# fp32 products in the long convolutions of a two-block network, low parts of keys copied by ScalarE, and another hand-out of the filter's tap tiles

## The chip, the cores and the metric

One core of a Trainium2 chip runs the whole program. The metric is device time in microseconds of one execution. TensorE (PE) multiplies, VectorE (DVE) and ScalarE (ACT) do elementwise work, GpSimd (POOL) does a few additions, and all loads and stores are issued by the queue of SyncE (SP). A run with the profiler gives a trace with one record per instruction.

## The reference

Two blocks of two layers each, in fp32, for 512 tokens and 256 context tokens of width 1024. What bears on the change is in the first block's layer 0: beside attention, half of the width goes through a "Hyena" operator, a gated long convolution of order 2:

```python
z = u[0]                                    # 512 channels
for o in range(HYENA_ORDER):                # 2 orders
    k = filters[o] / norm                   # taps in both directions, from a small MLP
    z = gate[o] * (fft_conv(z, k[o]) + skip[o] * z)
```

The kernel makes the convolution with products with cosine and sine matrices, for the 512 tokens and again for the 256 context tokens. The keys of all attentions (also in the second block) are rotated, normalised and multiplied with queries in the usual way.

## The kernel before, in words

An fp32 number is held as two `float32r` tiles: `h`, a rounded copy that ACT makes (`split`, L54), and `lo`, the rest that DVE makes (L55). One fp32-like product is then three matmuls (`mm3`, L81 to L83: high by high, high by low, low by high). A few products are single matmuls on plain fp32 tiles: `ada` (L161), `hy_mlp` (L466), the column sums in `hy_taps` (L556), `neigh` (L1027), and the transposes (L87).

Tiles come from rings by tag: `a` has 24 buffers, `oa` 6, `u` 4 (each holds two 1024-column halves), `st` 4 (landing place of weights that are then split), `e` 6, `va` 4. A new tile waits until a buffer of its ring is released. The tile framework orders the instructions of each engine, and each engine then runs its own in that order; all DMAs stand in one queue, that of SP. `merge` interleaves two generators in proportion to the costs that they yield, so the order of the program is set by these written-out costs.

Layer 0 (`layer0`, L826) has these stages around the change:

- Filters, 0 to 260 us: `hy_mlp`, `hy_kernels(1)` (context) and `hy_kernels(0)`, interleaved with `inputs` (norms, transposes, and `hy_in`, 12 weight units that go through the `u` ring). `hy_kernels` calls `hy_taps` for (o, hf) = (0,0), (0,1), (1,0), (1,1), and after each but the first the `hy_spec` of the one before it. `hy_taps` makes the tap tiles `E`: for the 512-token filter and hf 0 (of both orders) four tiles from `oa`, else two from `u`. `hy_spec` reads them, and they are released after it. `oa` also gives `new_y`: two tiles `yx` and one `yc`, written at L647 from `hy_in` unit 8 on.
- Projections and attention, 260 to 480 us. `k_pair` (L103) turns a pair of key heads in PSUM into `h` and `l` tiles with each head's rows in both halves of the partitions. For each head: two copies on ACT (L106, L107) and two subtractions on DVE (L108, L109). It is called 26 times in the whole kernel, to 2520 us.
- `hyena(1, ...)` (context) interleaved with the last gates, then `hyena(0, ...)` interleaved with `ctx_out` (the context's output projection, its norm and transposes, and two chunks of `ada`), 480 to 650 us. `hyena` (L663) loads z into `st` and splits it (L674), loads the DFT matrices into `st` and splits them (`dft`, L504; into `a` for the forward ones and one `u` each for the two inverse ones), and then for each order and each frequency block: forward products into PSUM tag `S` (L689, L691), sums and differences (L692, L693), the product with the filter's spectrum (L697 to L701), sum and difference of the two halves (L707) and the split of each (L708). Then the inverse products: order 0 at L724 with the matrix as stationary operand, times the gate (L726) and split into the next z (L727); order 1 at L740, with z-blocks as stationary operand.
- `out_proj` of the 512 tokens, from 645 us on, then layer 1 and the second block.

Of the kernel before, what the change touches and what calls it, by code (L numbers as in the profile page):

```python
# [9 lines left out]
F = mybir.dt.float32  # L10
R = mybir.dt.float32r
I32 = mybir.dt.int32
OP = mybir.AluOpType
AF = mybir.ActivationFunctionType
AX = mybir.AxisListType
P = 128
# [11 lines left out]
class Net:  # L28
# [74 lines left out]
    def k_pair(self, ps, Ah, Al, Bh, Bl):  # L103
        a, v = self.nc.scalar, self.nc.vector
        for s, h, l in ((slice(0, 64), Ah, Al), (slice(64, 128), Bh, Bl)):
            a.activation(h[0:64], ps[s], AF.Copy)  # L106
            a.activation(h[64:128], ps[s], AF.Copy)  # L107
            v.tensor_tensor(l[0:64], ps[s], h[s].bitcast(F), op=OP.subtract)  # L108
            v.tensor_tensor(l[64:128], ps[s], h[s].bitcast(F), op=OP.subtract)  # L109

    def av4(self, o, blocks, first, last):

# [403 lines left out]
    def hy_taps(self, o, hf, ni, w3, C):  # L516

        nc, I = self.nc, self.I
        b0, nb = ((0, 4), (4, 2))[ni]
        n = nb * P  # L520
        hs = self.hst
        wh, wl = w3
        ch = slice(hf * 256, (hf + 1) * 256)
        if ni == 0 and hf == 0:
            E = [self.t('oa', [P, 2, 2, 256], R) for _ in range(nb)]
        else:
            ts = [self.t('u', [P, 2, 2, 2, 256], R) for _ in range(nb // 2)]
            E = [ts[b // 2][:, b % 2] for b in range(nb)]
        acc = self.t('ec', [P, 2, 256])
        for b in range(nb):  # L530
            d = C['dec'][b // 2][:, b % 2, ch]
            ps = self.ps('S')
            for j in range(2):
                c = slice((b0 + b) * P, (b0 + b + 1) * P)
                p = ps[:, j * 256:(j + 1) * 256]
                nc.tensor.matmul(p, hs[:, c], wh[:, j, ch], start=True, stop=False)
                nc.tensor.matmul(p, hs[:, c], wl[:, j, ch], start=False, stop=b > 0)
                if b == 0:

# [24 lines left out]
        nc.scalar.activation(y, y, AF.Copy, scale=-0.5 / n)  # L564
        C[o, hf, ni] = E, y
        yield 1.5
# [67 lines left out]
    def hy_in(self, w, i0, streams):  # L634
# [3 lines left out]
        for m in range(12):  # L638
            u = self.wu(w, i0 + m)
            for h, nt, ctx, y in streams:  # L640
# [19 lines left out]
                    nc.sync.dma_start(self.zscr[ctx][m // 4][:, :, cs], v.rearrange("p (b c) -> p b c", c=P))  # L660
                yield 5.6 * nt / 4

    def hyena(self, ctx, y):  # L663

        nc = self.nc
        n = 256 if ctx else 512
        nh = n // 256
        nb = 2 * nh
        zs_ = []
        for b2 in range(nh):  # L670
            st = self.t('st', [P, 2, 512])
            hi, lo = self.t('a', [P, 2, 512], R), self.t('a', [P, 2, 512], R)
            nc.sync.dma_start(st, self.zscr[ctx][0][:, 2 * b2:2 * b2 + 2])
            self.split(hi, lo, st)  # L674
            zs_.append((hi, lo))
        for o in range(2):
            F4 = [self.dft(j) for j in range(2)] if n == 512 else [self.dft(4)]
            UV = []
            inv = [self.dft(2 + j, 'u') for j in range(2)] if n == 512 else F4 * 2
            for fb in range(nh):  # L680
                K, K1 = self.t('a', [P, 2, 512]), self.t('a', [P, 2, 512])
                for j, k in enumerate((K, K1)):
                    nc.sync.dma_start(k, self.kscr[2 if ctx else fb, o, j])

                def z(b):
                    return zs_[b // 2][0][:, b % 2], zs_[b // 2][1][:, b % 2]
                Z, Z1 = self.t('a', [P, 2, 512]), self.t('a', [P, 2, 512])
                for j in range(2):
                    B = self.dft_fwd(n, 2 * j + 1, fb, z, F4)  # L689
                    nc.scalar.activation(Z1[:, j], B, AF.Copy)  # L690
                    A = self.dft_fwd(n, 2 * j, fb, z, F4)  # L691
                    nc.vector.tensor_tensor(Z[:, j], A, Z1[:, j], op=OP.add)  # L692
                    nc.vector.tensor_tensor(Z1[:, j], A, Z1[:, j], op=OP.subtract)  # L693
                yield 5.1 * nh / 2
                for z_, k in ((Z1, K1), (Z, K)):
                    t1, t2 = self.t('e', [P, 512]), self.t('e', [P, 512])
                    nc.vector.tensor_tensor(t1, z_[:, 0], k[:, 1], op=OP.mult)  # L697
                    nc.vector.tensor_tensor(t2, z_[:, 1], k[:, 0], op=OP.mult)
                    nc.vector.tensor_tensor(z_, z_, k, op=OP.mult)
                    nc.vector.tensor_tensor(z_[:, 0], z_[:, 0], z_[:, 1], op=OP.subtract)  # L700
                    nc.vector.tensor_tensor(z_[:, 1], t1, t2, op=OP.add)  # L701
                uv = []
                for cs in range(2):
                    h, lo = self.t('a', [P, 2, 512], R), self.t('a', [P, 2, 512], R)
                    for j, op in enumerate((OP.add, OP.subtract)):
                        v = self.t('e', [P, 512])
                        nc.vector.tensor_tensor(v, Z[:, cs], Z1[:, cs], op=op)  # L707
                        self.split(h[:, j], lo[:, j], v)  # L708
                    uv.append((h, lo))
                UV.append(uv)  # L710

            if o == 0:
                zn = [(self.t('a', [P, 2, 512], R), self.t('a', [P, 2, 512], R)) for _ in range(nh)]
                for b in range(nb):
                    par, hf = b // nh, b % nh
                    p1 = self.t('va', [P, 512])
                    nc.sync.dma_start(p1, self.zscr[ctx][1][:, b])
                    ps = self.ps('S')
                    for fb in range(nh):
                        for cs in range(2):  # L720
                            u = inv[cs]
                            c = (fb * 2 + par) * 256 + hf * P if n == 512 else 512 + cs * 256 + par * P
                            h, lo = UV[fb][cs]
                            self.mm3(ps, u[0][:, c:c + P], u[1][:, c:c + P], h[:, par], lo[:, par],  # L724
                                     cs == 0 and fb == 0, cs == 1 and fb == nh - 1)
                    nc.vector.tensor_tensor(p1, ps, p1, op=OP.mult)  # L726
                    self.split(zn[b // 2][0][:, b % 2], zn[b // 2][1][:, b % 2], p1)  # L727
                    yield 2.6 * nh / 2
                zs_ = zn
            else:  # L730
                w2 = n // 2
                for cb in range(4):
                    ps = self.ps('pt')
                    ch = slice(cb * P, (cb + 1) * P)
                    for fb in range(nh):
                        for cs, par in ((0, 0), (0, 1), (1, 0), (1, 1)):
                            u = inv[cs]
                            c = (fb * 2 + par) * 256 if n == 512 else 512 + cs * 256 + par * P
                            h, lo = UV[fb][cs]
                            self.mm3(ps[:, par * w2:(par + 1) * w2], h[:, par, ch], lo[:, par, ch],  # L740
                                     u[0][:, c:c + w2], u[1][:, c:c + w2], fb + cs + par == 0, fb == nh - 1 and cs + par == 2)
                    yt = y[cb // 2][:, cb % 2].rearrange("p (t two) -> p two t", two=2)
                    nc.vector.tensor_tensor(yt, ps[:, :n].rearrange("p (two t) -> p two t", two=2), yt, op=OP.mult)
                    yield 2.6 * nh / 2
# [1472 lines left out]
```

## Time and profile before

| | us |
|---|---|
| median of 3 runs | 2936.05 (2933.27 to 2937.53) |
| the profiled execution | 2934.61 |
| its span, first to last instruction | 2932.8 |
| TensorE busy | 2795.8 (95%), 14904 matmuls |
| VectorE busy | 1974.4 (67%) |
| ScalarE busy | 1383.5 (47%) |
| mean granted clock of TensorE | 0.986 |

A matmul's record lasts longer than it holds the array, since its way through the array overlaps the next one's; the distance from start to start in a dense row of like matmuls is what one costs. An fp32 matmul on plain tiles stands in the trace as two records. In the tables of the profile "idle before" is the time that an engine sat idle ahead of such instructions, and behind the arrow stands what ended it.

### The profile page before, as it was taken

Reading aid. Unit: us, or ns where it says so; the run is one execution under the profiler, and the core shown is the slowest. Engines: PE = TensorE matmul, PEld = TensorE weight load, DVE = VectorE, ACT = ScalarE, POOL = GpSimd, SP = SyncE. Lnnn points to the kernel's source line nnn. Section 1 sums busy time; section 2 is a strip of 40 time slices with the busy share of each in tenths; the row PEclk is TensorE's granted clock in tenths of the full one; section 3 lists DMA queues with packets and bytes.
Section 4 is the critical chain, followed back from the end, with each engine's and each line's share of the span. In section 5 each row is a group of like instructions: output and inputs, shape, how many; then the busy total and the mean of one; then the engine's idle time right before and its main releaser. Section 6 shows DMA issues by size and latency. Waiting matters only on the chain.

```text
span 2932.8 us, 40392 instructions
## 1 busy us (share of the span) xinstructions
PE 2795.8 (95%) x14904; PEld 2278.0 (78%) x14904; DVE 1974.4 (67%) x4467; ACT 1383.5 (47%) x2843; POOL 124.6 (4%) x182
## 2 busy tenths in 40 slices
PE   7999999889999899999999899999999999899998
PEld 3888847558898687877788788888787778788886
DVE  5768868986978747876847734346877764954445
ACT  5544565334466625655635422234566543632322
POOL 0000000111001120100000000000100000000000
PEclk8999999999999999999999999999999999999999
DMA  6443142653214232222143222223221124233321
GB/s 230 137 127 96 39 130 94 207 187 114 75 62 138 78 129 79 87 73 65 58 152 101 80 101 94 86 101 122 68 94 58 58 79 144 87 95 107 101 94 65
DMA packets 117645, 299.77 MB, mean 102 GB/s; under 512 B 21471, under 2 KB 48031, under 8 KB 117448
## 3 DMA queue, kind: packets, MB, share of 16 engines
q1 hardware_dynamic: 117448, 297.19, 31.3%
q8 instruction: 118, 1.93, 0.3%
q14 instruction: 79, 0.65, 0.1%
HBM read 273.54 MB, written 27.54 MB: 103 GB/s over the span
## 4 chain that ended last, share of the span: by engine, by line
PE 75%; DVE 15%; ACT 5%; issue 2%; DMA 2%; SPq 0%; POOL 0%; ACTq 0%; DVEq 0%
PE mm L82 17%; PE mm L81 17%; PE mm L83 17%; PE pt L87 6%; DVE u L55 2%; PE o L121 2%; PE o L122 2%; PE o L161 1%; PE S L83 1%; PE S L81 1%; PE S L82 1%; PE mm L161 1%; PE o L1027 1%; DVE a L55 1%; PE S L1633 1%
## 5 line engine op out<-in xcount | busy, mean ns | idle before, releaser
L81 PE MATMUL mm<-a,u 128*128 128x512 f32 (+1 forms) x1596 | 592.6, 372 | 3.1 <-ACT a L54 1.4
L82 PE MATMUL mm<-a,u 128*128 128x512 f32 (+1 forms) x1596 | 591.3, 371 | 0.7 <-DVE a L55 0.7
L83 PE MATMUL mm<-a,u 128*128 128x512 f32 (+1 forms) x1596 | 588.8, 369 | 1.0 <-DVE u L55 1.0
L54 ACT ACTIVATE u<-st 128x1024 fp32r<-128x1024 f32 x352 | 369.0, 1051 | 383.3 <-PE mm L83 333.1
L55 DVE TENSOR_TENSOR u<-st,u 128x1024 fp32r<-128x1024 f32 x352 | 432.0, 1229 | 141.7 <-ACT u L54 135.9
L81 PE MATMUL mm<-u,a 128*128 128x512 f32 (+1 forms) x1280 | 458.9, 359 | 7.7 <-DVE v L778 3.2
L82 PE MATMUL mm<-u,a 128*128 128x512 f32 (+1 forms) x1280 | 458.7, 358 | 4.1 <-DVE u L55 4.0
L83 PE MATMUL mm<-u,a 128*128 128x512 f32 (+1 forms) x1280 | 457.2, 357 | 0.2 <-DVE a L58 0.2
L81 PEld LDWEIGHTS mm<-a,u 128*128 128x128 f32 x1596 | 301.5, 189 | 52.5 <-ACT a L54 2.4
L83 PEld LDWEIGHTS mm<-a,u 128*128 128x128 f32 x1596 | 301.4, 189 | 49.1 <-DVE u L55 1.8
L82 PEld LDWEIGHTS mm<-a,u 128*128 128x128 f32 x1596 | 301.7, 189 | 47.8 <-issue 2.1
L81 PEld LDWEIGHTS mm<-u,a 128*128 128x128 f32 x1280 | 242.6, 190 | 44.3 <-DVE v L778 3.5
L82 PEld LDWEIGHTS mm<-u,a 128*128 128x128 f32 x1280 | 242.8, 190 | 39.8 <-DVE u L55 6.4
L83 PEld LDWEIGHTS mm<-u,a 128*128 128x128 f32 x1280 | 242.7, 190 | 34.5 <-DVE a L58 1.0
L55 DVE TENSOR_TENSOR va<-pt,va 128x512 fp32r<-128x512 f32 (+2 forms) x252 | 165.3, 670 | 67.2 <-ACT va L54 55.1
L1207 DVE SCALAR_TENSOR_TENSOR a<-a,mm 128x512 f32<-128x512 f32 x96 | 65.7, 685 | 210.3 <-PE mm L83 210.2
L87 PE MATMUL pt<-c_ident,e 128*128 128x128 f32 x1132 | 188.4, 278 | 18.7 <-DVE e L274 3.7
L54 ACT ACTIVATE va<-pt 128x512 fp32r<-128x512 f32 (+2 forms) x252 | 143.2, 583 | 122.7 <-PE pt L87 113.0
L87 PEld LDWEIGHTS pt<-c_ident,e 128*128 128x128 f32 x1132 | 133.7, 141 | 65.3 <-issue 20.4
L1892 DVE TENSOR_TENSOR v<-v 128x512 f32<-128x512 f32 x64 | 44.3, 693 | 160.4 <-ACT v L1891 159.9
L1891 ACT ACTIVATE v<-mm 128x512 f32<-128x512 f32 x60 | 36.0, 600 | 203.0 <-PE mm L83 203.0
L82 PE MATMUL S<-u,a 128*128 128x256 f32 x312 | 91.0, 292 | 1.5 <-DVE u L55 1.5
(424 smaller groups left out, 4827.7 us busy)
## 6 DMA issues: line engine op xcount, KB each, us to landing
st<-in_up SPq DMA_DIRECT2D x64, 512.0 KB
st<-in_dn SPq DMA_DIRECT2D x64, 512.0 KB
st<-in_w SPq DMA_DIRECT2D x52, 512.0 KB
st<-in_ada SPq DMA_DIRECT2D x48, 512.0 KB
st<-in_gate SPq DMA_DIRECT2D x48, 512.0 KB
st<-in_win SPq DMA_DIRECT2D x42, 512.0 KB
st<-in_wout SPq DMA_DIRECT2D x24, 512.0 KB
st<-in_br SPq DMA_DIRECT2D x16, 512.0 KB
```

The lines of the kernel that those rows point to most:

```text
L54: nc.scalar.activation(hi, src, AF.Copy)
L55: (eng or nc.vector).tensor_tensor(lo, src, hi.bitcast(F), op=OP.subtract)
L81: mm(ps, ah, bh, start=first, stop=False)
L82: mm(ps, ah, bl, start=False, stop=False)
L83: mm(ps, al, bh, start=False, stop=last)
L87: self.nc.tensor.transpose(dst, src, self.ident[:n, :n])
L121: nc.tensor.matmul(o, v, ph[:nk], start=first and bi == 0, stop=False)
L122: nc.tensor.matmul(o, v, pl[:nk], start=False, stop=last and bi == len(blocks) - 1)
L161: nc.tensor.matmul(ps[:nr], cc[:, 2 * kk + j], v[:, j * 512:(j + 1) * 512], start=kk + j + x == 0, stop=2 * kk + j == 7 and x == len(w) - 1)
L1207: self.nc.vector.scalar_tensor_tensor(xx, xx, alpha, ps, op0=OP.mult, op1=OP.add, **kw)
L1891: nc.scalar.activation(r, ps, AF.Relu)
L1892: nc.vector.tensor_tensor(sq, r, r, op=OP.mult)
```

## The change

Three edits. In `hyena`, z, the DFT matrices, the two halves of the spectrum product and the next z are kept as plain fp32 tiles without a split, and each `mm3` there becomes one matmul on fp32 tiles (`dft_fwd32` for the forward one). The loads go straight into the tiles that the matmuls read; both inverse matrices share one `u` tile. `hy_spec` keeps `dft`, `dft_fwd` and `mm3`. In `k_pair`, the second subtraction of each head becomes an ACT copy of the first one's result into the other half of the partitions. In `hy_taps`, of the 512-token filter only (0,1) takes its tap tiles from `oa`; (0,0) and (1,0), which did before, take two `u` tiles each, and (0,1), which took `u`, no longer does.

```diff
@@ k_pair
-            v.tensor_tensor(l[0:64], ps[s], h[s].bitcast(F), op=OP.subtract)
-            v.tensor_tensor(l[64:128], ps[s], h[s].bitcast(F), op=OP.subtract)
+            v.tensor_tensor(l[s], ps[s], h[s].bitcast(F), op=OP.subtract)
+            a.activation(l[64 - s.start:128 - s.start], l[s].bitcast(F), AF.Copy)
@@ hy_taps
-        if ni == 0 and hf == 0:
+        if ni == 0 and (o, hf) == (0, 1):
             E = [self.t('oa', [P, 2, 2, 256], R) for _ in range(nb)]
@@ new
+    def dft_raw(self, j):
+        t_ = self.t('a', [P, 1024])
+        self.nc.sync.dma_start(t_, self.I['dft'][j])
+        return t_
+    def dft_pair(self):
+        u = self.t('u', [P, 2, 1024])
+        for j in range(2):
+            self.nc.sync.dma_start(u[:, j], self.I['dft'][2 + j])
+        return [u[:, 0], u[:, 1]]
+    def dft_fwd32(self, n, m, fb, z, F4, ps=None):
...
+        for hf in range(nh):
...
+            self.nc.tensor.matmul(ps, u[:, c:c + P], z(par * nh + hf), start=hf == 0, stop=hf == nh - 1)
+        return ps
@@ hyena
-            st = self.t('st', [P, 2, 512])
-            hi, lo = self.t('a', [P, 2, 512], R), self.t('a', [P, 2, 512], R)
-            nc.sync.dma_start(st, self.zscr[ctx][0][:, 2 * b2:2 * b2 + 2])
-            self.split(hi, lo, st)
-            zs_.append((hi, lo))
+            z_ = self.t('a', [P, 2, 512])
+            nc.sync.dma_start(z_, self.zscr[ctx][0][:, 2 * b2:2 * b2 + 2])
+            zs_.append(z_)
...
-            F4 = [self.dft(j) for j in range(2)] if n == 512 else [self.dft(4)]
+            F4 = [self.dft_raw(j) for j in ((0, 1) if n == 512 else (4,))]
-            inv = [self.dft(2 + j, 'u') for j in range(2)] if n == 512 else F4 * 2
+            inv = self.dft_pair() if n == 512 else F4 * 2
...
-                    B = self.dft_fwd(n, 2 * j + 1, fb, z, F4)
+                    B = self.dft_fwd32(n, 2 * j + 1, fb, z, F4)
...
-                    h, lo = self.t('a', [P, 2, 512], R), self.t('a', [P, 2, 512], R)
+                    v = self.t('a', [P, 2, 512])
                     for j, op in enumerate((OP.add, OP.subtract)):
-                        v = self.t('e', [P, 512])
-                        nc.vector.tensor_tensor(v, Z[:, cs], Z1[:, cs], op=op)
-                        self.split(h[:, j], lo[:, j], v)
+                        nc.vector.tensor_tensor(v[:, j], Z[:, cs], Z1[:, cs], op=op)
...
-                            self.mm3(ps, u[0][:, c:c + P], u[1][:, c:c + P], h[:, par], lo[:, par],
-                                     cs == 0 and fb == 0, cs == 1 and fb == nh - 1)
-                    nc.vector.tensor_tensor(p1, ps, p1, op=OP.mult)
-                    self.split(zn[b // 2][0][:, b % 2], zn[b // 2][1][:, b % 2], p1)
+                            nc.tensor.matmul(ps, u[:, c:c + P], UV[fb][cs][:, par],
+                                             start=cs == 0 and fb == 0, stop=cs == 1 and fb == nh - 1)
+                    nc.vector.tensor_tensor(zn[b // 2][:, b % 2], ps, p1, op=OP.mult)
...
-                            self.mm3(ps[:, par * w2:(par + 1) * w2], h[:, par, ch], lo[:, par, ch],
-                                     u[0][:, c:c + w2], u[1][:, c:c + w2], fb + cs + par == 0, fb == nh - 1 and cs + par == 2)
+                            nc.tensor.matmul(ps[:, par * w2:(par + 1) * w2], UV[fb][cs][:, par, ch], u[:, c:c + w2],
+                                             start=fb + cs + par == 0, stop=fb == nh - 1 and cs + par == 2)
```

## Rows read from the trace of the kernel before

**Rows 1.** The page: busy time of each engine, share of the span, instructions

```profile
...
PE 2795.8 (95%) x14904; PEld 2278.0 (78%) x14904; DVE 1974.4 (67%) x4467; ACT 1383.5 (47%) x2843; POOL 124.6 (4%) x182
...
```

**Rows 2.** Busy time by engine (x instructions), PEclk, DMA share, GB/s; the hyena stretch

```profile
...
500.00:650.00 150.00, 127.08 (x532) 83.22 (x530) 138.81 (x198) 63.14 (x95) 17.44 (x8) 0.94 0.58 199
...
```

**Rows 3.** The chain of waits of 500 to 660 us, shares by line

```profile
...
by line: DVE a L55 7.4%; DVE u L55 7.3%; issue 7.0%; DMA st<-in_wout 6.8%; PE o L161 6.3%; DVE a L699 5.0%; DVE e L707 4.7%; DVE a L700 3.8%; DMA a<-kscr 3.7%; DVE e L698 3.2%; DVE e L697 3.1%; DVE a L58 2.9%; PE S L83 2.8%; PE mm L82 2.6%;
...
```

**Rows 4.** Groups by line and form, 480 to 650 us: splits

```profile
...
L55 DVE TENSOR_TENSOR u<-st,u 128x1024 fp32r<-128x1024 f32 x15 | 19.3, 1293 | 3.6 <-ACT u L54 3.5
...
L55 DVE TENSOR_TENSOR a<-e,a 128x512 fp32r<-128x512 f32 x24 | 17.7, 777 | 1.4 <-ACT a L54 1.4
...
L54 ACT ACTIVATE a<-e 128x512 fp32r<-128x512 f32 x24 | 14.8, 629 | 34.2 <-DVE e L707 34.2
...
L55 DVE TENSOR_TENSOR a<-st,a 128x1024 fp32r<-128x1024 f32 x7 | 8.4, 1216 | 0.0
...
L55 DVE TENSOR_TENSOR a<-va,a 128x512 fp32r<-128x512 f32 x6 | 6.2, 1044 | 0.0
...
```

**Rows 5.** The same view: first matmul of each three-part product in hyena

```profile
...
L81 PE MATMUL S<-a,a 128*128 128x512 f32 x44 | 19.3, 442 | 2.5 <-ACT a L54 2.4
...
L81 PE MATMUL pt<-u,a 128*128 128x256 f32 x32 | 10.0, 315 | 8.9 <-ACT a L54 8.3 <-DVE oa L743 0.7
...
L81 PE MATMUL S<-a,u 128*128 128x512 f32 x16 | 6.1, 404 | 0.0
...
L81 PE MATMUL pt<-a,a 128*128 128x128 f32 x16 | 4.4, 283 | 0.9 <-ACT a L54 0.9
...
```

**Rows 6.** Timeline of TensorE: start, length, line, tiles, form; dense rows of like matmuls

```profile
...
103.97 1.02 PE L556 MATMUL o<-ec,ones 128*128 128x256 f32 x4
...
110.32 0.28 PE L82 MATMUL mm<-a,u 128*128 128x256 f32 x1
110.44 0.28 PE L83 MATMUL mm<-a,u 128*128 128x256 f32 x1
...
515.76 7.03 PE L161 MATMUL o<-st,c 128*2 128x512 f32 x16 [0.68 <-ACT v L165]
...
527.34 0.28 PE L82 MATMUL pt<-a,a 128*128 128x128 f32 x1
527.45 0.28 PE L81 MATMUL pt<-a,a 128*128 128x128 f32 x1
...
556.16 0.39 PE L82 MATMUL mm<-u,a 128*128 128x512 f32 x1
556.39 0.39 PE L83 MATMUL mm<-u,a 128*128 128x512 f32 x1
...
949.87 1.09 PE L1027 MATMUL o<-va,a 128*64 128x128 f32 x8
...
```

**Rows 7.** Waits, 600 to 650 us: who, for whom, total us, times, longest

```profile
...
PE pt L81 <- ACT a L54: 8.3, 1, 8.3
...
```

**Rows 8.** Timeline of VectorE at the last split in hyena

```profile
...
637.84 0.69 DVE L55 TENSOR_TENSOR a<-e,a 128x512 fp32r<-128x512 f32 x1 [0.70 <-ACT a L54]
...
```

**Rows 9.** DMA queue: start, time in the queue; four DFT loads of order 1

```profile
...
565.30 17.56 SPq L507 DMA_DIRECT2D st<-in_dft  x4
...
```

**Rows 10.** Waits, 570 to 600 us, columns as in Rows 7

```profile
...
ACT u L54 <- PE mm L83: 11.1, 2, 10.6
...
```

**Rows 11.** Line L109 of k_pair: durations in ns min/median/max; who waited for it

```profile
...
L109 DVE TENSOR_TENSOR a<-pt,a x28: 417/428/695, 269.6 to 1007.4; 64x256 fp32r<-64x256 f32 x20, 64x512 fp32r<-64x512 f32 x8
...
  PEld mm L81: 3.4, 4
...
```

**Rows 12.** Line L107, the second copy of k_pair on ScalarE

```profile
...
L107 ACT ACTIVATE a<-pt x28: 375/378/593, 268.3 to 1006.6; 64x256 fp32r<-64x256 f32 x20, 64x512 fp32r<-64x512 f32 x8
...
```

**Rows 13.** End of the filters, columns as in Rows 2

```profile
...
220.00:230.00 10.00, 7.16 (x41) 6.60 (x41) 8.01 (x13) 6.02 (x11) 0.00 (x0) 0.73 0.28 68
...
```

**Rows 14.** Timeline of ScalarE: the gate unit that waits for its oa tile

```profile
...
232.80 0.78 ACT L647 ACTIVATE oa<-mm,c_hyc 128x512 f32<-128x512 f32 x1 [1.98 <-PE S L83]
```

More of the change, by code (lines that the diff above doesn't have):

```diff
@@ L661, in hy_in @@
                 yield 5.6 * nt / 4
+    def dft_raw(self, j):
[8 more added lines that the diff above has]
+    def dft_fwd32(self, n, m, fb, z, F4, ps=None):
+        par, sin = m % 2, m // 2
+        if ps is None:
+            ps = self.ps('S')
+        nh = n // 256
+        for hf in range(nh):
+            if n == 512:
+                u, c = F4[sin], (par * 2 + hf) * 256 + fb * P
+            else:
+                u, c = F4[0], sin * 256 + par * P
+            self.nc.tensor.matmul(ps, u[:, c:c + P], z(par * nh + hf), start=hf == 0, stop=hf == nh - 1)
+        return ps
     def hyena(self, ctx, y):
@@ L685, in z @@
                 def z(b):
-                    return zs_[b // 2][0][:, b % 2], zs_[b // 2][1][:, b % 2]
+                    return zs_[b // 2][:, b % 2]
                 Z, Z1 = self.t('a', [P, 2, 512]), self.t('a', [P, 2, 512])
                 for j in range(2):
-                    B = self.dft_fwd(n, 2 * j + 1, fb, z, F4)
+                    B = self.dft_fwd32(n, 2 * j + 1, fb, z, F4)
                     nc.scalar.activation(Z1[:, j], B, AF.Copy)
-                    A = self.dft_fwd(n, 2 * j, fb, z, F4)
+                    A = self.dft_fwd32(n, 2 * j, fb, z, F4)
                     nc.vector.tensor_tensor(Z[:, j], A, Z1[:, j], op=OP.add)
@@ L703, in hyena @@
                 for cs in range(2):
-                    h, lo = self.t('a', [P, 2, 512], R), self.t('a', [P, 2, 512], R)
+                    v = self.t('a', [P, 2, 512])
                     for j, op in enumerate((OP.add, OP.subtract)):
-                        v = self.t('e', [P, 512])
-                        nc.vector.tensor_tensor(v, Z[:, cs], Z1[:, cs], op=op)
-                        self.split(h[:, j], lo[:, j], v)
-                    uv.append((h, lo))
+                        nc.vector.tensor_tensor(v[:, j], Z[:, cs], Z1[:, cs], op=op)
+                    uv.append(v)
                 UV.append(uv)
             if o == 0:
-                zn = [(self.t('a', [P, 2, 512], R), self.t('a', [P, 2, 512], R)) for _ in range(nh)]
+                zn = [self.t('a', [P, 2, 512]) for _ in range(nh)]
                 for b in range(nb):
@@ L722, in hyena @@
                             c = (fb * 2 + par) * 256 + hf * P if n == 512 else 512 + cs * 256 + par * P
-                            h, lo = UV[fb][cs]
-                            self.mm3(ps, u[0][:, c:c + P], u[1][:, c:c + P], h[:, par], lo[:, par],
-                                     cs == 0 and fb == 0, cs == 1 and fb == nh - 1)
-                    nc.vector.tensor_tensor(p1, ps, p1, op=OP.mult)
-                    self.split(zn[b // 2][0][:, b % 2], zn[b // 2][1][:, b % 2], p1)
+                            nc.tensor.matmul(ps, u[:, c:c + P], UV[fb][cs][:, par],
+                                             start=cs == 0 and fb == 0, stop=cs == 1 and fb == nh - 1)
+                    nc.vector.tensor_tensor(zn[b // 2][:, b % 2], ps, p1, op=OP.mult)
                     yield 2.6 * nh / 2
@@ L738, in hyena @@
                             c = (fb * 2 + par) * 256 if n == 512 else 512 + cs * 256 + par * P
-                            h, lo = UV[fb][cs]
-                            self.mm3(ps[:, par * w2:(par + 1) * w2], h[:, par, ch], lo[:, par, ch],
-                                     u[0][:, c:c + w2], u[1][:, c:c + w2], fb + cs + par == 0, fb == nh - 1 and cs + par == 2)
+                            nc.tensor.matmul(ps[:, par * w2:(par + 1) * w2], UV[fb][cs][:, par, ch], u[:, c:c + w2],
+                                             start=fb + cs + par == 0, stop=fb == nh - 1 and cs + par == 2)
                     yt = y[cb // 2][:, cb % 2].rearrange("p (t two) -> p two t", two=2)
```

## The prediction, made before the changed kernel was seen

> **What bounds the kernel now.** I read the page first: over the whole span TensorE is busy 95%, VectorE 67%, ScalarE 47% [rows 1]. By that alone, work added to TensorE would be added to the end. But the kernel has stages with different limits, so I next read busy time by stretches. In the 150 us that hold most of `hyena` (500 to 650 us) the order is turned: TensorE 127.1 us, VectorE 138.8, ScalarE 63.1 (first, third and fourth figure of the row) [rows 2]. VectorE is the fullest engine, with 93%, and TensorE stands unused for at least 22.9 us. At least, because a lone matmul's record lasts 0.39 us where it holds the array for 0.23. The chain of waits of 500 to 660 us says the same from the other side: its two largest shares are the splits at L55, 7.4% into `a` tiles and 7.3% into `u` tiles; the loads of the output projection's weights have 6.8% [rows 3].
>
> **fp32 products in hyena: what goes.** All its splits. On VectorE: the 24 halves of the spectrum product, 17.7 us; the z and DFT splits into `a`, 7 in this stretch, 8.4 us; the new z, 6, 6.2 us; and of the 15 splits into `u` the four that are inverse DFT matrices, 4 x 1.29 = 5.2 us [rows 4]. Together 37.5 us (two more DFT splits lie before 480 us and are free there). ScalarE loses one copy for each, 14.8 us for the 24 halves [rows 4] and about as much again for the rest; it was under half full, so I give that nothing for itself. VectorE is left with 138.8 - 37.5 = 101.3 us in 150.
>
> **What comes.** `hyena` has 44 + 16 products of 512 columns, 32 of 256 and 16 of 128 [rows 5]; a row counts the first of three matmuls. From start to start a `float32r` matmul costs 0.23 us at 512 columns, 0.12 at 256 and 0.11 at 128. An fp32 matmul stands there as two records: sixteen of 512 columns take 7.03 us, 0.43 each without the tail of 0.16; four of 256 take 1.02, 0.215 each; eight of 128 take 1.09, 0.117 each [rows 6]. So one product goes from 3 x 0.23 = 0.69 to 2 x 0.43 = 0.86 at 512 columns, from 0.36 to 0.43 at 256, from 0.33 to 0.23 at 128. The sum is 60 x 0.17 + 32 x 0.07 - 16 x 0.10 = 10.2 + 2.2 - 1.6 = **10.8 us more on TensorE**. The row of sixteen has only two stationary columns. The row of four has 128, and its price per column is the same, so I add nothing for weight loads; there are also two loads in place of three.
>
> The rows show a plain fp32 product as two records that cost 1.25 times the three-part one. The Trainium skill ("FP8 and Floating Point Precision", section TensorE Precision Notes) counts four passes through the array for true fp32. By that, with today's cost per pass, the sum would be 60 x 0.23 + 32 x 0.12 + 16 x 0.11 = 19.4 us, 8.6 us more than by the rows, and the forecast that much later. I keep to the rows.
>
> **What of it moves the end.** Two bounds. By load: TensorE would hold 127.1 + 10.8 = 137.9 of 150 us and be the fullest, so if the work packs, the stretch loses 12.1 us, and more as far as lone records overstate its work. By the chain: 7.4% of 160 us is 11.8, and 4 of 15 of the 7.3% is 3.1, so 14.9 us of splits leave the path [rows 3]; the copies that ScalarE makes ahead of them leave it too. The clearest place is the end of order 1: TensorE waits 8.3 us in one piece for ScalarE's copy [rows 7], and behind that copy VectorE's last split waits 0.70 and takes 0.69 [rows 8]. In place of these, products on the path grow by a quarter; the chain gives `S` products only a few per cent, so 1 to 2 us. I take **-14 us**. Low end -24: all VectorE time in excess goes, and TensorE's granted clock, 0.94 of full as a mean here [rows 2], no longer falls to its lower level (1.2 GHz) after pauses. High end -4: what is late next takes the rest, that is the weights' loads, the spectrum products L697 to L701, and transfers at 199 GB/s as a mean.
>
> **Loads.** The same 13 tiles (8 + 2 DFT, 3 z) are loaded, but into the ring they are used from. Before, order 1's four DFT loads spent 17.6 us in SP's queue for `st` buffers [rows 9], with the `ada` weights and the filter spectra queued behind them, and ScalarE stood up to 10.6 us before a `u` buffer that TensorE still read, with other copies behind it [rows 10]. Now SP waits for an `a` or a `u` buffer. Per 512-token order `hyena` needs about 18 `a` buffers (there are 24) in place of 28, and one `u` in place of two, so these waits should be shorter, not longer. I price this at nothing beyond the chain's sum. If an `a` buffer is late, all loads behind stand still: a cost of one weight unit, some 5 us, kept for the range.
>
> **k_pair.** 52 VectorE instructions of 0.43 us (256 columns) or 0.69 (512) go [rows 11], 22 to 36 us in all, and 52 ScalarE copies of about 0.38 or 0.59 come [rows 12]. Most lie beside a full TensorE. TensorE's queue waited 3.4 us in all for L109 at the largest such place [rows 11]. The second head's copies can start one VectorE instruction earlier, while the first head's new copy may stand before them on ScalarE; the two nearly cancel. I take **-1 us**, between -5 (all such waits and some room on VectorE in the attention stages) and +5 (26 calls, 0.2 us of longer path in each).
>
> **Tap tiles.** Before, (1,0) holds four of six `oa` buffers while `yx` and `yc` want three: the evacuation of `hy_in`'s unit 10 for the 512 tokens stands at 232.8 us, released by the spectrum matmuls that free `oa` [rows 14]. In 220 to 230 us TensorE is busy 7.2 of 10 us at a mean clock of 0.73 [rows 13]: a pause, and matmuls at the lower level after it. With (0,1) in `oa` instead, its buffers come free with the spectrum of (0,1), before unit 10. In return (1,0) and (1,1) take all four `u` at the end of the filters, and unit 11 (24 x 0.23 + 24 x 0.12 = 8.4 us of matmuls) and the first attention weights find none until the spectrum of (1,0) is done. That work must be done in any case; only what TensorE can't fill is lost. I take **-2 us**, between -6 (pause and low clock both gone) and +9 (unit 11 alone at the end).
>
> **Sum.** -14 - 1 - 2 = -17 us against the profiled execution's 2934.6: 2917.6. The median of the runs is 1.4 us above it, so **2919 us**.
>
> **Rivals.**
> 1. *The freed time lands in the next wait.* VectorE's splits go, but the weights' loads (6.8% of the chain, 10.9 us [rows 3]) and the chain spectrum, product, inverse are then what TensorE waits for. For: DMA share 0.58 in the stretch [rows 2]. Against: the loads themselves stood in queues behind split buffers. Time: hyena -4, nothing else: 2932 us.
> 2. *TensorE is the bound after all, slower.* In each frequency block the products stand on the path and TensorE has no other work ready, so that its pauses cannot take the 10.8 us; every product's growth is paid, and the splits were only hidden beside it. Place: 500 to 645 us. Price: +10.8, gain of splits 0: 2947 us. It decides from the point where VectorE without splits still has a product's operands ready before TensorE is done with the one before. For: 95% on the page [rows 1]. Against: 22.9 us unused in the stretch [rows 2] and an 8.3 us wait for a copy [rows 7]. The Trainium skill has this as a rule ("Perfetto Trace Analysis", Identifying the Most-Contended Engine): the most-contended engine is the one with the highest occupancy, and that one is to be optimised first; over the whole span that is TensorE. The stretch's row speaks against it here.
> 3. *The `u` ring starves at the end of the filters.* hyena -14, k_pair -1, but unit 11 and the first attention weights come late, +9 and 3 for two splits on ScalarE and VectorE: 2933 us.
>
> **How the numbers follow.** Forecast 0.70, its own range 2905 to 2930 (hyena -24 to -9, the two others -5 to +4). Rival 1 0.13, rival 2 0.08, rival 3 0.09. About 0.2% (5.9 us) is what a measurement of this kernel can tell from no change, so the bounds are 2930 and 2942. Faster: nearly all of the forecast, a third of rival 1, a third of rival 3: 0.76. Slower: rival 2, 0.08. Same: 0.16. The range that leaves out two in ten reaches into rivals 1 and 3 but not to rival 2: 2903 to 2936.
>
> **What the changed profile would show.** In the hyena stretch no L55 or L54 but for weights, fp32 matmuls in pairs 0.43 us apart, VectorE near 75%, TensorE its fullest engine and `out_proj` of the 512 tokens beginning some 17 us earlier, 14 of them from this stretch. In `k_pair` one VectorE and three ScalarE instructions per head. At 215 to 235 us no wait of L647. I am wrong if fp32 matmuls with 128 stationary columns lie further apart than 0.43 us, if `out_proj` begins less than 5 us earlier, or if the gain is there at 650 us and lost again in the attention stages after it.

## The result and the profile after

The changed kernel takes 2903.9 us (median of 4 runs, 2901.0 to 2906.0) against 2934.7 us before in the same job: a ratio of 0.9893, interval 0.9877 to 0.9908, or 30.8 us. Timed a second time (the last experiment) it took 2902.0, ratio 0.9902 (0.9888 to 0.9915). The forecast was 17 us. The direction held, the size did not.

Busy time over the span, on the page of the changed kernel (its counterpart is [rows 1]):

```profile
PE 2800.0 (96%) x14796; PEld 2263.0 (78%) x14796; DVE 1912.3 (66%) x4372; ACT 1380.1 (48%) x2852; POOL 122.3 (4%) x182
```

VectorE lost 62 us of work, and TensorE's busy time grew by 4. By the page VectorE still looks like an engine with a third of its time free; the experiments show that taking work off it paid all the same.

Where the time went is read by setting the starts of like instructions of the two traces against each other (median difference at some moments of the kernel before, us; minus is earlier):

| at (us) | what lies before it | changed kernel | fp32 products alone | k_pair alone | tap tiles alone | changed, k_pair undone |
|---|---|---|---|---|---|---|
| 262 | filters | -2.2 | -2.7 | -0.3 | -2.3 | -4.6 |
| 480 | projections, attention | -6.0 | -3.9 | -3.4 | -4.6 | -8.3 |
| 645 | hyena | -19.7 | -18.1 | -4.8 | +5.4 | -20.9 |
| 850 | out_proj, next projections | -21.7 | -18.9 | -6.8 | +4.7 | -20.3 |
| 1061 | neighbourhood attention | -26.5 | -19.2 | -11.7 | +4.7 | -19.7 |
| 1900 | second block, first half | -28.4 | -19.4 | -14.0 | +3.5 | -20.0 |
| 2900 | rest | -29.4 | -17.2 | -15.1 | +4.0 | -20.0 |

In `hyena` 13.7 us are gained (480 to 645), as forecast. What the forecast lacks comes in small steps, all in stages where `k_pair` is called: 3.8 us from 262 to 480, 2.0 by 850, 4.8 by the end of the neighbourhood attention, 2.9 later. The first of them can't be put down to `k_pair`: the changed kernel with `k_pair` undone (last column; it is one of the experiments) gains 3.7 us there too, and nothing behind `hyena`. (Two profiled executions of the changed kernel itself differ by 3.5 us at 262 us, 2.1 at 1061 and 5.0 at the end, so a step of 2 or 3 us says little by itself.)

The hyena stretch of the changed kernel, columns as in [rows 2]:

```profile
490.00:628.00 138.00, 132.73 (x451) 70.56 (x450) 108.47 (x163) 34.76 (x55) 10.47 (x7) 1.00 0.60 211
```

The order of the engines has turned: TensorE 96% (85% before), VectorE 79% (93%), and the granted clock is 1.00, so 2.4 GHz throughout, in place of a mean of 0.94. Before, TensorE ran at its lower level, 1.2 GHz, in four stretches of 17.2 us together, and was busy for 13.8 of them (columns as in [rows 2]):

```profile
528.40:531.90 3.50, 3.50 (x11) 2.68 (x11) 3.46 (x5) 0.62 (x1) 0.00 (x0) 0.51 0.91 265
562.60:566.00 3.40, 3.40 (x9) 2.64 (x9) 3.40 (x4) 0.24 (x1) 0.95 (x1) 0.50 0.00 0
593.30:596.70 3.40, 3.40 (x7) 1.50 (x6) 3.30 (x9) 0.76 (x1) 0.00 (x0) 0.50 0.78 237
630.80:637.70 6.90, 3.46 (x15) 3.25 (x16) 6.34 (x10) 2.36 (x4) 0.00 (x0) 0.51 0.69 243
```

At the full clock that work would have taken about half as long, so by an estimate from these rows some 7 us of the stretch's gain are the clock's. Dense rows of fp32 products on TensorE's timeline (start, length, line, tiles, form, count):

```profile
495.13 3.59 PE L746 MATMUL S<-a,a 128*128 128x512 f32 x8
...
517.96 2.05 PE L760 MATMUL pt<-a,a 128*128 128x128 f32 x16
...
614.95 10.82 PE L760 MATMUL pt<-u,a 128*128 128x256 f32 x48
```

Less the last one's tail of about 0.16 that is (3.59 - 0.16) / 8 = 0.43, 1.89 / 16 = 0.12 and 10.66 / 48 = 0.22 us per record: the prices of [rows 6], with 128 stationary columns. In place of TensorE waiting for ScalarE's copies [rows 7], VectorE now waits for TensorE (waits of the stretch 494 to 630: who, for whom, total, times, longest):

```profile
DVE a L717 <- PE S L687: 10.6, 3, 8.5
...
DVE oa L763 <- PE pt L760: 6.8, 6, 2.1
...
PE mm L82 <- DVE u L55: 1.9, 2, 1.7
```

The DFT loads no longer stand in their queue: SP's queue with the same matrices, against 17.56 us in [rows 9].

```profile
515.20 0.92 SPq L666 DMA_DIRECT2D a<-in_dft  x2
...
567.58 1.02 SPq L673 DMA_DIRECT2D u<-in_dft  x2
570.64 0.89 SPq L666 DMA_DIRECT2D a<-in_dft  x2
```

Eight loads of output-projection weights still do (18.5 us in that queue, 16.4 before), and ScalarE waited 16.5 us for them in place of 5.9; but TensorE waited no more than 2.6 us in all for the splits behind them.

At the end of the filters the pause of [rows 13, 14] is gone: no L647 stands at 232 us, and TensorE is busy all of 220 to 230 us, at clock 1.00.

```profile
220.00:230.00 10.00, 10.00 (x83) 9.89 (x82) 9.85 (x18) 7.14 (x12) 0.00 (x0) 1.00 0.24 57
```

Last, `k_pair`. The answer for L109 from which [rows 11] are taken has more lines, which the prediction left out, the longest wait among them. Four of them, the same kernel before:

```profile
  ACT a L106: 22.6, 14
...
  PE mm L81: 2.2, 4
  PEld S L1010: 1.4, 1
  PE S L1010: 1.0, 1
```

After the change L106 waits for no VectorE instruction (first fence: what L106 waited for; second: what VectorE's remaining subtraction L108 waited for; third: who waited for that subtraction):

```profile
  PE mm L83: 9.2, 6
  PE pt L87: 8.0, 5
```

```profile
  ACT a L107: 15.9, 17
```

```profile
  ACT a L109: 12.4, 16
```

L109 is now ScalarE's copy of the low part, and stands ahead of the second pair of copies. So ScalarE's wait for VectorE in `k_pair` fell from 22.6 to 12.4 us, and at first sight that is the gain. The experiments were made to test that, among other things.

### The profile page after: what moved, and what is told of

It reads as the page before. It is cut to its first block, busy times and chain, and to the rows that moved or that the text cites. A ratio compares the mean times of both kernels' runs of the same rounds, so it can differ in the third digit from the quotient of the medians.

```text
span 2903.6 us, 40076 instructions
## 1 busy us (share of the span) xinstructions
PE 2800.0 (96%) x14796; PEld 2263.0 (78%) x14796; DVE 1912.3 (66%) x4372; ACT 1380.1 (48%) x2852; POOL 122.3 (4%) x182
## 4 chain that ended last, share of the span: by engine, by line
PE 55%; DVE 7%; ACT 3%; issue 1%; DMA 1%; ACTq 0%; DVEq 0%
PE mm L81 15%; PE mm L82 15%; PE mm L83 15%; PE pt L87 3%; PE o L121 1%; PE o L122 1%; PE S L1653 1%; DVE u L55 1%; PE S L1654 1%; DVE a L1158 1%; PE S L1423 1%; DVE a L1162 1%; DVE va L55 1%; PE o L1513 1%; ACT u L54 0%
## 5 line engine op out<-in xcount | busy, mean ns | idle before, releaser
L54 ACT ACTIVATE u<-st 128x1024 fp32r<-128x1024 f32 (+1 forms) x348 | 364.6, 1051 | 398.9 <-PE mm L83 356.8
L55 DVE TENSOR_TENSOR u<-st,u 128x1024 fp32r<-128x1024 f32 (+1 forms) x348 | 426.5, 1227 | 143.2 <-ACT u L54 137.0
L55 DVE TENSOR_TENSOR va<-pt,va 128x512 fp32r<-128x512 f32 (+2 forms) x252 | 165.2, 669 | 62.3 <-ACT va L54 54.1
L54 ACT ACTIVATE va<-pt 128x512 fp32r<-128x512 f32 (+2 forms) x252 | 142.9, 582 | 117.7 <-PE pt L87 107.7
```

The lines of the kernel that those rows point to most:

```text
L54: nc.scalar.activation(hi, src, AF.Copy)
L55: (eng or nc.vector).tensor_tensor(lo, src, hi.bitcast(F), op=OP.subtract)
```

## The experiments

All times are medians; the ratio is that to the kernel before, timed on the same chip in the same job (2932.8 in the first, then 2932.5, 2933.9 and 2932.0).

**1. The parts, one by one.** Theory A: the parts add, each in its own stages. Theory B: `k_pair` is worth 1 us, and the rest follows from `hyena`.

The fp32 products alone: the kernel before with `hyena`, `dft_raw`, `dft_pair` and `dft_fwd32` of the change.

> The kernel before with the fp32 products in hyena alone. The two traces put the changed kernel 15.7 us closer at the end of the hyena stretch than at its start, and some 6 us more are gained at later stages that hold k_pair. Theory A (parts add up; each gain belongs to the edit of its own stage): -16 us against before, about 2918.5. Theory B (k_pair is worth the 1 us that was forecast, and the later gains follow from the hyena edit through a shifted schedule): -27 us, about 2908. By A the shift against before is some -15 at 650 us and stays there; by B it grows by 6 us or more between 850 and 1110 us.

Measured: 2917.6, ratio 0.9951 (0.9939 to 0.9964), -14.4 us. The shift stays at -19 from 650 to 1900 us, as A has it.

`k_pair` alone:

```diff
-            v.tensor_tensor(l[0:64], ps[s], h[s].bitcast(F), op=OP.subtract)
-            v.tensor_tensor(l[64:128], ps[s], h[s].bitcast(F), op=OP.subtract)
+            v.tensor_tensor(l[s], ps[s], h[s].bitcast(F), op=OP.subtract)
+            a.activation(l[64 - s.start:128 - s.start], l[s].bitcast(F), AF.Copy)
```

> The kernel before with the edit of k_pair alone. Theory A: -11 us, about 2924, in steps of some 3.5 us at 260 to 480 us, 5 at 910 to 1060 us, and 3 in the second block. Theory B: -1 us, about 2934. In both, the second head's first ACT copy no longer waits for the second subtraction on DVE (22.6 us of ACT idle time in 14 places before).

Measured: 2919.7, ratio 0.9959 (0.9945 to 0.9973), -12.0 us. A holds, B falls; the largest step, 4.9 us, is that of the neighbourhood attention.

The tap tiles alone:

```diff
-        if ni == 0 and hf == 0:
+        if ni == 0 and (o, hf) == (0, 1):
```

> The kernel before with the tap tiles handed out in the other order alone. Theory A and theory B: -2 us, about 2932.5, all of it by 265 us. A third theory, that the early gain of 2.5 us is only borrowed and given back where the gates of the next stage are waited for: 0 us, about 2934.7.

Measured: 2938.6, ratio 1.0017 (1.0008 to 1.0025), 5.0 us slower: neither. By the table it is 4.6 us ahead at 480 us and loses 10 in `hyena`, where nothing of the edit runs. There TensorE's order had changed: of its 14592 instructions 788 stand elsewhere than before, up to `hyena` and not behind it, because the framework orders the program anew for every source. In that order the loads of z and of the DFT matrices come late, one behind the other. Lines of the chain of waits in this kernel, 505 to 545 us (start, length, what):

```profile
516.22 4.77 DMA st<-z
521.00 0.02 issue
521.02 1.06 ACT a L54
522.08 0.02 issue
522.11 1.24 DVE a L55
523.36 3.63 DMA st<-in_dft
```

Each load waits for the split that frees an `st` buffer. TensorE pauses twice, and then runs at half its clock (columns as in [rows 2]):

```profile
521.00:524.00 3.00, 1.09 (x9) 0.81 (x8) 2.19 (x4) 2.63 (x3) 0.00 (x0) 1.00 0.15 60
524.00:533.00 9.00, 9.00 (x32) 6.30 (x33) 5.01 (x7) 3.17 (x3) 0.00 (x0) 0.51 0.74 244
```

Pauses of 1.9 us in all and 9 us at 0.51: by estimate some 6 us there.

The changed kernel with `k_pair` undone (the diff above, turned round):

> The changed kernel with the second subtraction of k_pair back on DVE. Theory A: about 11 us slower than the changed kernel, 2915. Theory B: 1 us slower, 2905. By A the shift against the changed kernel appears at 260 to 480 us (3 to 4 us), 910 to 1060 us (some 5 us) and in the second block (some 3 us).

Measured: 2913.7, ratio 0.9936 (0.9923 to 0.9948), 9.8 us more than the changed kernel. A again in the sum: `k_pair` is worth 10 to 12 us in either company. But the step expected at 260 to 480 us, where 6 of the 52 instructions stand, did not come: by the table's columns this run keeps pace with the changed kernel there (0.1 us), and loses 1.1 in `hyena`, 2.6 by 850, 5.4 by 1061 and 2.6 behind.

**2. Why `k_pair` is worth that.** Theory C: ACT and DVE take turns at one PSUM tile, and the change ends a turn earlier. Theory D: it is VectorE's time.

Both heads' copies ahead of all subtractions, VectorE's load as before:

```diff
         for s, h, l in ((slice(0, 64), Ah, Al), (slice(64, 128), Bh, Bl)):
             a.activation(h[0:64], ps[s], AF.Copy)
             a.activation(h[64:128], ps[s], AF.Copy)
-            v.tensor_tensor(l[s], ps[s], h[s].bitcast(F), op=OP.subtract)
-            a.activation(l[64 - s.start:128 - s.start], l[s].bitcast(F), AF.Copy)
+        for s, h, l in ((slice(0, 64), Ah, Al), (slice(64, 128), Bh, Bl)):
+            v.tensor_tensor(l[0:64], ps[s], h[s].bitcast(F), op=OP.subtract)
+            v.tensor_tensor(l[64:128], ps[s], h[s].bitcast(F), op=OP.subtract)
```

> The changed kernel with k_pair's two subtractions per head back on DVE, but with both heads' four ACT copies ahead of all four subtractions. With k_pair undone the changed kernel took 2913.7, 10 us more than the 2903.9 it takes itself. Theory C (the 10 us were ACT's second pair of copies standing behind the first head's second subtraction, since ACT and DVE read the same PSUM bank by turns): the wait is gone and all or most of the gain stays, 2904 to 2907, though DVE has 52 more instructions. Theory D (the 10 us are DVE's load, 52 instructions of 0.43 or 0.69 us): as with k_pair undone, 2913.

Measured: 2929.0, ratio 0.9989 (0.9980 to 0.9998), 25 us more than the changed kernel, worse than both theories. ScalarE's wait is gone, as meant. In its place VectorE stands before ScalarE's fourth copy (what its first subtraction, here L109, waited for):

```profile
  ACT a L107: 26.6, 15
```

The low part's copy on VectorE:

```diff
-            a.activation(l[64 - s.start:128 - s.start], l[s].bitcast(F), AF.Copy)
+            v.tensor_copy(l[64 - s.start:128 - s.start], l[s].bitcast(F))
```

> The changed kernel with the copy of the low part into the other half of the partitions on DVE in place of ACT (from SBUF, so DVE reads PSUM only once per head). Theory C: the second head's first ACT copy still starts after one subtraction, so the gain stays, 2904 to 2907. Theory D: DVE has its 52 instructions back, 2910 to 2914, less if a copy from SBUF is shorter on DVE than a subtraction with a PSUM operand (0.43 and 0.69 us).

Measured: 2910.9, ratio 0.9927 (0.9914 to 0.9939), 7 us more. The copy is shorter than a subtraction (durations min/median/max in ns, line L109 of this kernel):

```profile
L109 DVE CAST a<-a x52: 285/292/839, 264.2 to 2496.4; 64x256 fp32r<-64x256 f32 x28, 64x512 fp32r<-64x512 f32 x24
```

After these, D was mended to: what counts is the time that VectorE spends in `k_pair`, at work or waiting, since its queue stands behind. The test was an instruction of VectorE that takes nothing but time:

```diff
             v.tensor_tensor(l[s], ps[s], h[s].bitcast(F), op=OP.subtract)
             a.activation(l[64 - s.start:128 - s.start], l[s].bitcast(F), AF.Copy)
+            v.tensor_reduce(self.dum[s], l[s].bitcast(F), axis=AX.X, op=OP.min)
...
+            self.dum = self.cn.tile([P, 1], F, name='dum')
```

> The changed kernel with one more DVE instruction per head in k_pair, at the place where the second subtraction stood: a reduction over the first one's result, which nothing reads (52 instructions, some 0.3 us at 256 columns and 0.6 at 512, about 23 us in all). ACT keeps its copies, and PSUM is read by DVE only once per head. Theory C (PSUM's turns between ACT and DVE): as the changed kernel, 2904 to 2906. Theory D, as mended by the last runs (what counts is DVE's time in k_pair, its instructions and its waits there: 44.2 us in the changed kernel, 58.6 with the copies on DVE, 70.6 with k_pair undone, 83.2 with all ACT copies first, and 2903.9, 2910.9, 2913.7 and 2929.0 us): about 44 + 23 = 67 us on DVE, 2910 to 2914.

Measured: 2912.8, ratio 0.9928 (0.9914 to 0.9941), 9 us more. So C is not enough: here ScalarE's second copies wait for no VectorE instruction, the low part's copy ahead of them waits 12.1 us (12.4 in the changed kernel), nothing waits for the reduction, and yet nearly all of `k_pair`'s gain is gone. The run is less clean than it was meant to be, though: set against the changed kernel, 989 of TensorE's 14796 matmul records stand elsewhere in its order, 349 of them in the neighbourhood attention.

| k_pair as | VectorE at work in it + waiting for ACT (us) | time (us) |
|---|---|---|
| changed kernel | 28.3 + 15.9 = 44.2 | 2903.9 |
| copy on VectorE | 47.4 + 11.2 = 58.6 | 2910.9 |
| useless reduction | 56.1 + 12.0 = 68.1 | 2912.8 |
| undone | 56.7 + 13.9 = 70.6 | 2913.7 |
| all ACT copies first | 56.6 + 26.6 = 83.2 | 2929.0 |

The first number is the sum of its records there, the second the wait before its first subtraction. One can see where time is lost in the neighbourhood attention, the stage with the largest step. Before, TensorE is busy 151 of 165 us there, and VectorE 125, 76% (columns as in [rows 2]):

```profile
895.00:1060.00 165.00, 151.27 (x956) 122.75 (x955) 125.35 (x329) 96.89 (x196) 30.23 (x45) 1.00 0.35 101
```

Waits of TensorE and ScalarE there, in the kernel before (895 to 1060 us), with `k_pair` alone changed (888 to 1048), in the changed kernel with the reduction (878 to 1045) and with all copies first (878 to 1051):

```profile
ACT e L1017 <- DVE sma L1014: 7.5, 7, 3.3
PE o L1027 <- ACT va L1024: 7.1, 11, 1.2
```

```profile
ACT e L1017 <- DVE sma L1014: 2.0, 4, 0.9
PE o L1027 <- ACT va L1024: 0.5, 1, 0.5
```

```profile
ACT e L1038 <- DVE sma L1035: 3.2, 6, 1.0
PE o L1048 <- ACT va L1045: 3.7, 7, 0.7
```

```profile
ACT e L1038 <- DVE sma L1035: 18.9, 12, 5.6
PE o L1048 <- ACT va L1045: 6.0, 10, 0.7
PE S L1029 <- DVE sma L1035: 5.0, 3, 2.8
```

TensorE waits for ScalarE's eviction of transposed weights (L1024, L1045), which comes behind a softmax with steps on VectorE: first VectorE's sum with the bias (L1014, L1035), for which ScalarE's exponential (L1017, L1038) waits. TensorE stands unused for 13.7 us of the stage before, 6.4 with `k_pair` alone changed, 10.8 with the reduction and 15.7 with all copies first.

What stays open: these edits also move instructions (770 of TensorE's in the run with `k_pair` alone), and how much of the 10 us is VectorE's time itself and how much the order that comes with it was not separated. With the reduction the exponential waits hardly longer than with `k_pair` alone (3.2 us against 2.0), while TensorE's wait for L1045 is 3.7 against 0.5, so the order may have a large part in that run.

GpSimd for the copy, meant to beat the changed kernel:

```diff
-            a.activation(l[64 - s.start:128 - s.start], l[s].bitcast(F), AF.Copy)
+            self.nc.gpsimd.tensor_copy(l[64 - s.start:128 - s.start], l[s].bitcast(F))
```

> The changed kernel with the copy of the low part on GpSimd in place of ACT. ACT loses 52 copies, 26.8 us, and its second pair of copies no longer stands behind a copy that waits for DVE; DVE's waits for ACT in k_pair (15.9 us) should shrink. By theory D: -3 us, about 2901. If GpSimd's copy is much longer than ACT's 0.42 and 0.63 us, TensorE waits for it: +2 to +8 us, 2906 to 2912.

Measured: 2909.5, ratio 0.9917 (0.9903 to 0.9930), 6 us more. VectorE's time in `k_pair` is 40.8 us, so D alone would have it faster. By its medians the copy is no longer than ScalarE's (0.40 and 0.61 us at 256 and 512 columns against 0.42 and 0.63), but it is uneven, up to 2.59 us, and TensorE waits for it, at L1030 4.1 us in place of 1.4 (L109, and two lines of who waited for it):

```profile
L109 POOL CAST a<-a x52: 392/610/2587, 268.2 to 2498.4; 64x256 fp32r<-64x256 f32 x28, 64x512 fp32r<-64x512 f32 x24
...
  PEld S L1030: 4.1, 5
  PEld S L1803: 3.9, 2
```

**3. Why `hyena` gains.** Theory E: it is VectorE's load. Theory F: it is the chain of copy and split ahead of each product. VectorE's load put back without its chain:

```diff
                         nc.vector.tensor_tensor(v[:, j], Z[:, cs], Z1[:, cs], op=op)
+                        nc.vector.tensor_tensor(self.t('e', [P, 512]), v[:, j], Z[:, cs], op=OP.subtract)
```

> The changed kernel with 24 useless subtractions of 128x512 on DVE in hyena, one behind each half of the spectrum product, whose results nothing reads: about 24 x 0.69 = 16.6 us of DVE time put back, without a wait for ACT and without the ring of the split tiles. Theory E (hyena's gain of 14 us came from DVE's load): 5 to 12 us slower than the changed kernel, 2909 to 2916. Theory F (it came from the chain of ACT's copy and DVE's split ahead of each product and from the loads' ring): 0 to 3 us slower, 2904 to 2907.

Measured: 2908.0, ratio 0.9917 (0.9903 to 0.9931): 4 us more by the medians, 7 by the ratios. The 24 took 15.5 us, and the shift against the changed kernel grows by 5.5 us between 480 and 645 us: the low end of E. So a third of a VectorE microsecond comes out in the end here, though TensorE is the fuller engine. Here TensorE's order hardly changed: 72 of its records stand elsewhere, all in this stage. That the chain (F) has the rest was not tested by itself.

The same edit where TensorE does not pause, plain fp32 for the filter's spectrum as well:

```diff
...
+        Et = self.t('u', [P, nb, 2, 256])
+        E = [Et[:, b] for b in range(nb)]
...
-            self.split(E[b][:, 0], E[b][:, 1], v)
...
-                    self.dft_fwd(n, 2 * j + m, f, lambda b: (E[b][:, 0, j], E[b][:, 1, j]), F4, ps[:, m * 256:(m + 1) * 256])
+                    self.dft_fwd32(n, 2 * j + m, f, lambda b: E[b][:, j], F4, ps[:, m * 256:(m + 1) * 256])
...
```

> The changed kernel with the filter spectrum's products in plain fp32 too: the tap tiles are not split any more and take one u tile instead of two or of four oa tiles, and the DFT matrices are loaded straight into a. 24 splits of taps and 3 of matrices leave ACT and DVE in the first 260 us; about 80 products of 256 columns grow by 0.07 us, 5.6 us on TensorE. If that stretch is like hyena's, where TensorE paused for splits: -3 to -8 us, 2896 to 2901. If TensorE is full there: +3 to +6, 2907 to 2910.

Measured: 2923.4, ratio 0.9968 (0.9956 to 0.9981), 19 us more. TensorE is busy all of 200 to 230 us in the changed kernel; the end of the filters comes 7 us later by 262 us, where the expectation's sum for the longer products was 5.6, and 10 more are lost by 480 us, in pauses with a low clock (columns as in [rows 2]). The edit also gives each set of tap tiles one `u` tile, so what the longer products alone cost is not separated.

```profile
250.00:260.00 10.00, 7.45 (x34) 6.74 (x35) 9.45 (x14) 2.08 (x4) 4.26 (x3) 0.66 0.40 129
...
270.00:280.00 10.00, 4.60 (x39) 4.39 (x37) 7.37 (x30) 3.12 (x6) 0.00 (x0) 0.93 0.00 0
280.00:290.00 10.00, 7.15 (x38) 7.15 (x39) 6.74 (x26) 3.18 (x9) 0.00 (x0) 0.56 0.79 276
```

**4. The tap tiles in other company.** The changed kernel without that edit, the kernel before with it and `k_pair`, and the changed kernel once more:

```diff
-        if ni == 0 and (o, hf) == (0, 1):
+        if ni == 0 and hf == 0:
```

> The changed kernel with the tap tiles handed out as before. From the runs without k_pair's edit, where the tap tiles took 3.9 us off beside the fp32 products (2917.6 to 2913.7): 2908. From the run with the tap tiles alone, which cost 5.8 us: 2898. If they are worth nothing in this company: 2904.

> The kernel before with the edits of k_pair and of the tap tiles, and hyena with its splits. The tap tiles cost 5.8 us alone (2938.6 against 2932.8), took 3.9 off beside the fp32 products, and 1.8 beside both others. Theory G (alone, the new order of the program lets the z and DFT loads of hyena stand one behind the other, each waiting for the split that frees its st buffer, and fp32 products take that chain away): it comes back as soon as hyena has its splits, about 2919.7 + 5.8 = 2925, with 8 us or so more than the run with k_pair alone between 480 and 650 us. Theory H (the 5.8 us are an accident of that one order, which another edit ahead of hyena shifts away): 2916 to 2920.

> The changed kernel itself, once more beside the same runs of the kernel before: 2903.9 by its first timing. The version without the tap tiles' edit took 2905.7 beside other runs (ratio 0.9905, with 0.9891 to 0.9918), so the edit's share is read as the difference of the two ratios: 0.9893 again would make it 0.12%, 3.5 us.

Measured: 2905.7, ratio 0.9905 (0.9891 to 0.9918); 2918.5, ratio 0.9952 (0.9939 to 0.9966); 2902.0, ratio 0.9902 (0.9888 to 0.9915). So the edit is worth +5.0 us alone, -4.4 beside the fp32 products, -2.1 beside `k_pair`, and -1 to -3.5 beside both (differences of the ratios, times 2933; each of the ratios has some 4 us of uncertainty to either side). Two signs are sure: the first, and the second by the runs themselves, which do not overlap (2912.4 to 2915.3 with the edit, 2916.2 to 2920.9 without, in one job). Theory G falls and H holds: with `hyena`'s splits still there, another edit ahead of it was enough to make the loss go; the run with `k_pair` and the tap tiles loses nothing to the one with `k_pair` alone from 480 to 645 us.

## Why the prediction was right in its direction and wrong in its size

- **Hyena, -14: right in size and direction, in part by luck.** The stretch gave -14.2 alone and -13.7 in the changed kernel. The prices of [rows 6] held. VectorE at 79% was near the forecast 75, TensorE is the fullest engine, and no L54 or L55 but those of weights is left there. But the clock rose to 1.00, which the sum had kept for its low end only, and some 7 of the 13.7 us are the clock's by the estimate above. With it the load bound would have been 127.1 - 6.9 + 10.8 = 131.0 us of TensorE (132.7 measured); the work did not pack to that, and 5.3 of the 138.0 us stand unused. Set against the bound of 12.1, these two nearly cancel. Putting VectorE's load back showed that the load has a part; the chain's part is argued only.
- **The rule on true fp32, four passes.** The Trainium skill ("FP8 and Floating Point Precision", TensorE Precision Notes) has it; the runs show a product of 512 columns at 2 x 0.43 = 0.86 us beside 0.23 for one `float32r` matmul, 3.7 times, but one of 128 columns at 0.24 beside 0.11, 2.1 times. So the count is about right at 512 columns, and what was off was to price each pass as a whole `float32r` matmul at every size; the rows' 10.8 us was the better sum.
- **Rival 1, the freed time lands in the next wait, fell:** ScalarE's wait for the weights' loads did grow, from 5.9 to 16.5 us, but `hyena` gave 13.7 us and not 4.
- **Rival 2, TensorE is the bound after all, fell in `hyena`:** -14.4 us against its +10.8. Its rule (the Trainium skill, "Perfetto Trace Analysis", Identifying the Most-Contended Engine) agrees with the trace in that stage, where VectorE was the fullest engine. In the neighbourhood attention it hangs on the measure: by matmul time TensorE was the fullest, 92% against VectorE's 76%, and work taken off VectorE still paid; by the time of its weight loads, by which the section has TensorE judged, it was at 74% (122.75 of 165 us).
- **Loads, 0: nothing speaks against it.** The queue's 17.56 us became 1.9 for the same four DFT loads; what that alone was worth no run shows. ScalarE's longest wait for a `u` buffer [rows 10] did not get shorter, 12.7 us against 10.6.
- **k_pair, -1: this is the step that failed.** It measured -12.0 alone and -9.8 as an undo, well outside its bounds of -5 and +5. The sentence that failed is "Most lie beside a full TensorE": the price was taken from who waited for L109 directly, 3.4 us of TensorE, and the rest of VectorE's 28 us was taken as covered. TensorE is not full in the stage with the largest step (151 of 165 us), and what it waits for there ends in chains that pass through VectorE's queue: its wait for L1024 fell from 7.1 to 0.5 us, and ScalarE's for L1014 ahead of that from 7.5 to 2.0. "The two nearly cancel" failed as well: ScalarE's wait for VectorE fell from 22.6 to 12.4 us. That wait is not enough as a cause, since runs without it at L106 lost most of the gain. How much is VectorE's time and how much the new order of instructions stays open. With -10 to -12 for this term the sum would be -26 to -28; the 3 to 5 us that are left to 30.8 are no larger than the uncertainty of the terms.
- **Tap tiles, -2: right in the changed kernel** (-1 to -3.5), with the pause of [rows 13, 14] gone as said; rival 3 did not come. But the term was an accident in one respect that the prediction did not see: the edit orders the whole first 650 us anew, and alone it ended at +5.0.
- **"Wrong if the gain is lost again in the attention stages":** the opposite came, 9.7 us were added from 645 us on.

## What to carry to other kernels

An engine at 76% beside another at 92% is not cover: don't price an instruction that goes by who waits for it directly, but follow what the fuller engine waits for back through the chain, and bound the term by the whole sum of what goes. Here 28 us taken off VectorE gave 10 to 12, and 15.5 us put back in `hyena` cost 5.5; the share of about a third is these two cases', and in the first the order of instructions changed along with it. Plain fp32 in place of a split into three products paid where the split's engines held TensorE up, and the one trial where TensorE was dense lost 19 us. Time every edit in the company in which it ships: the framework orders the program anew, and here one edit came out between -4 and +5 us.

## What the runs showed of the hardware that was not expected

- ScalarE's copy of the second head (partitions 64 to 127 of a PSUM tile) began at 927.53 us in the kernel before, as VectorE's subtraction from the first head (partitions 0 to 63, 926.81 + 0.69) ended, though both only read the tile. The trace has the copy waiting for a semaphore that the subtraction raises, so the program asks for this order; whether the hardware needs it isn't shown.
- On VectorE a copy of 64x256 from SBUF took 0.29 us, a subtraction with a PSUM operand 0.42, and a reduction of 64x256 to one column 0.41 (medians); GpSimd's copy of 64x256 took 0.39 to 2.59, with a median of 0.40.
- Pauses of TensorE of 1.9 us in all were followed, in the run with the tap tiles alone, by 9 us at a granted clock of 0.51, its lower level of 1.2 GHz: the pauses themselves were the smaller part of the loss, 1.9 us against some 4.4 by estimate (9 x 0.49).
